# Up projection of an MLP: three of four hidden groups as seven quarter products instead of eight, input normalised first, residual parked in memory

## The chip, the cores and the metric

One core of a Trainium2 chip runs the whole program. The metric is the device time of one execution in microseconds (us). Three runs of the kernel before gave 1219.78, 1217.89 and 1219.12 us; their median is 1219.12 us.

## The reference

One decoder layer is computed in float32 for 512 prompt tokens and 8 samples of 8 tokens: a token mixer, a cross attention into 256 memory tokens, and a squared-ReLU MLP with 4096 hidden columns. The change is in the MLP and in what leads into it:

```python
x = x + rmsnorm(cross_attn(rmsnorm(x, g_pre_xa), mem_k, mem_v, w_xq, w_xo), g_post_xa)
hf = rmsnorm(x, g_pre_ffn)
x = x + rmsnorm(jnp.square(jax.nn.relu(hf @ w_up)) @ w_down, g_post_ffn)
```

`w_up` is 1024 x 4096 and `w_down` is 4096 x 1024; there are 576 tokens in all.

## The kernel before, in words

Activations lie transposed, features on the 128 partitions, as tiles `[128, 8, 576]`: 8 slices of 128 features, the 576 tokens in two halves of 288. Every float32 operand is split into a high part (a cast, `split` L92 on ACT) and a low part (the rest, L93 on DVE), and every product of a weight tile and an activation slice is three matmuls of 128 x 128 by 288 columns: high by high, low by high, high by low (`mm3`, L197 to L200). One weight tile `[128, 1024]` holds 8 such blocks, the whole depth of 1024 for 128 output columns, so it is worth 24 matmuls for one half of the tokens.

Weights come by a plan that is fixed when the program is built (L132 to L163). `wfetch` (L166) loads the next 512 KB tile into one of four `wraw` buffers through SP's queue; `wsplit` (L175) makes `wh` and `wl` in a ring of three buffers; `wnext` (L187) keeps two split tiles ready. Side work is written as generators that `tick` (L117) advances by a step after each stretch of matmuls. `project` (L375) computes one half of the tokens at a time, and keeps a few split tiles of the first half for the second (`keep`; `KEEP_FFN` is 4), so the others are loaded and split again. `gemm_m` (L208) computes both halves with each tile.

The cross attention's output projection (`w_xo`) runs by halves (L506 to L524). While its second half runs, `chain_xa(0)` (L511) turns the first half into the MLP's input: `residual` (L420) computes the post norm's factor (`rstd` L228: sums of squares by three small matmuls L223, a power on POOL L236, a diagonal L240, a broadcast matmul L247), scales (L429), adds the residual (L431), and writes `fh` and `fl`, the input times its gain but **not** divided by its own root mean square (L438, L439). Squared ReLU is homogeneous, so that division is made at the end: `vff` keeps what the last norm needs for it (L518, L519, used at L234 to L238). `chain_xa(1)` does the same for the second half while the MLP has begun on the first.

The MLP (L531 to L557) takes the 4096 hidden columns in four groups of 1024. Each group is an up projection (group 0 by halves through `project`, groups 1 to 3 through `gemm_m`) whose eviction `to_h` (L535) applies ReLU on ACT, the square on DVE (L538) and the split, then a down projection that is summed over the groups in `y3` (L555, L557). The last group's down projection runs by halves in `last` (L559), each followed by the post norm, the residual and the store. The tiles `fh`, `fl` carry the program's names `bh`, `bl` in the profile, and the hidden tiles `xh`, `xl`.

The order in which each engine's instructions stand is fixed at build time by a scheduler that works from this code; each engine then runs its own row in order and waits on semaphores.

Of the kernel before, what the change touches and what calls it, by code (L numbers as in the profile page):

```python
# [6 lines left out]
F32 = mybir.dt.float32  # L7
# [49 lines left out]
def decoder_step(ctx, tc, xT, memT, ktc, vc, s_gla, s_ret, w_in, w_ga, w_a2, w_mix, w_xq, w_xk, w_xv, w_xo,  # L57
                 w_up, w_down, vecs, cst, gam, y_out, mk_out, mv_out, sg_p, sr_p, sg_s, sr_s):
# [20 lines left out]
    vff = [[perm.tile([96, 3], F32, name=f"vff{i}{j}") for j in range(2)] for i in range(2)]  # L79
# [5 lines left out]
    wz = acta.tile([P, 256], F32R, name="wz")  # L85
# [78 lines left out]
    raws, ready, staying = [], [], []  # L164

    def wfetch():  # L166
        if plan:
            src, mode = plan.pop(0), RING
            if isinstance(src, tuple):
                src, mode = src  # L170
            raw = wp.tile([P, 1024], F32, name="wraw", bufs=N_RAW)
            nc.sync.dma_start(out=raw if len(src.shape) == 2 else raw.rearrange("p (k n) -> p k n", n=src.shape[2]), in_=src)
            raws.append((raw, mode))

    def wsplit():  # L175
        if raws:
# [25 lines left out]
    def gemm(ps, w, xh, xl, c, k0=0, k1=KT):  # L202

        wh, wl = w
        for k in range(k0, k1):
            mm3(ps, wh[:, k, :], wl[:, k, :], xh[:, k, c], xl[:, k, c], k == 0, k == KT - 1)

    def gemm_m(xh, xl):  # L208
        w = wnext()
        ps = gtile()  # L210
        gemm(ps[:, 0, :NH], w, xh, xl, hc(0))
        tick()
        gemm(ps[:, 1, :NH], w, xh, xl, hc(1))
        return ps[:, :, :NH]

# [12 lines left out]
    def rstd(ss, n, t, v=None):  # L228


        ms = meansq(ss, n, t, EPS if v is None else 0.0)
        rs = npool.tile([P, 4], F32, name="rs")
        if v is not None:
            nc.vector.tensor_tensor(out=ms, in0=ms, in1=v[1], op=ALU.mult)  # L234
            nc.vector.tensor_scalar(out=ms, in0=ms, scalar1=EPS, scalar2=None, op0=ALU.add)  # L235
        nc.gpsimd.tensor_tensor(out=rs[:t, :n], in0=ms, in1=mhalf[:t, :n], op=ALU.pow)  # L236
        if v is not None:
            nc.vector.tensor_tensor(out=rs[:t, :n], in0=rs[:t, :n], in1=v[0], op=ALU.mult)  # L238
# [129 lines left out]
    y2p = ctx.enter_context(tc.tile_pool(name="y2p", bufs=1))  # L368
# [51 lines left out]
    def residual(y, r, half, ss, ss2=None, g2=None, oh=None, ol=None, scale=None, done=None):  # L420

        c = hc(half)
        rs, dg = rstd(ss, 3, 96, scale)
# [84 lines left out]
    fh = actb.tile([P, KT, NT], F32R, name="bh")  # L508
    fl = actb.tile([P, KT, NT], F32R, name="bl")

    def chain_xa(half):  # L511

        ss2 = y2p.tile([P, 2, 384], F32, name="ss2")
        yield from residual((y2a, y2b)[half], rr, half, ss[half], ss2[:, :, :NH], V_PRE_FFN, fh, fl)

        def stats():
# [3 lines left out]
        yield from stats()  # L520

    side.append(chain_xa(0))
    project(ah, al, 1, to(y2b, V_POST_XA, ss[1]))
    drain()  # L524
    side.append(chain_xa(1))


    hp = ctx.enter_context(tc.tile_pool(name="hp", bufs=2))
    staying.append(ctx.enter_context(tc.tile_pool(name="keepf", bufs=KEEP_FFN)))
    y3 = None  # L530
    for g in range(4):  # L531
        hh = acta.tile([P, KT, NT], F32R, name="xh")
        hl = acta.tile([P, KT, NT], F32R, name="xl")

        def to_h(hv, lv, ps):  # L535
            r = hp.tile([P, 2, NH], F32, name="hr")
            nc.scalar.activation(r, ps, AF.Relu)  # L537
            nc.vector.tensor_tensor(out=r, in0=r, in1=r, op=ALU.mult)  # L538
            split(hv, lv, r)

        if g == 0:
            for half in range(2):
                c = hc(half)
                project(fh, fl, half, lambda b, ps, first: to_h(hh[:, 2 * b:2 * b + 2, c], hl[:, 2 * b:2 * b + 2, c], ps), keep=KEEP_FFN)
                drain()
        else:
            for k in range(KT):
                to_h(h2(hh[:, k, :]), h2(hl[:, k, :]), gemm_m(fh, fl))
        if g == 0:
            y3 = biga.tile([P, KT, NT], F32, name="y3", tag="biga")  # L550
        if g < 3:
            for k in range(KT):
                ps = gemm_m(hh, hl)
                if g == 0:
                    nc.scalar.copy(h2(y3[:, k, :]), ps)  # L555
                else:
                    nc.vector.tensor_tensor(out=h2(y3[:, k, :]), in0=ps, in1=h2(y3[:, k, :]), op=ALU.add)  # L557

    def last(half):  # L559
# [20 lines left out]
        project(hh, hl, half, evict, keep=KEEP_FFN, end=end)  # L580

        def done(kk, c):
            nc.sync.dma_start(out=y_out[:, kk, c], in_=res[:, kk, c])
        side.append(residual(yv, rr, half, s1, scale=vff[half], done=done))
# [647 lines left out]
```

## Time and profile before

| | |
|---|---|
| median of three runs | 1219.12 us (1217.89 to 1219.78) |
| profiled execution, its own time | 1221.61 us |
| its span, first to last instruction | 1219.9 us |
| mean granted TensorE clock | 0.989 |
| PE busy | 1190.6 us, 98% of the span, 9130 matmuls |
| DVE, ACT, POOL busy | 696.9, 527.7, 154.5 us (57%, 43%, 13%) |
| chain of work that ended last | PE 90%, DMA 4%, DVE 2%, ACT 2% |

The span is the profiled execution from its first to its last instruction; 1.7 us of its time lie around it. A matmul's busy time is its way through the array, so busy times of matmuls overlap, and PE's pace is read from the starts of neighbouring matmuls. Shares of busy time are means over stages, and the stages differ; the windows of single stages tell more.

### The profile page before, as it was taken

How to read it: one execution, taken by the hardware profiler on the slowest of the kernel's cores; microseconds unless marked ns; L12 is line 12 of the kernel's file. 1: busy time of each engine (PE TensorE's matmuls, PEld its weight loads, DVE VectorE, ACT ScalarE, POOL GpSimd, SP SyncE). 2: the span in 40 equal slices, each digit the busy share in tenths (PEclk: the TensorE clock that was granted, in tenths of full speed). 3: DMA queues.
4: the chain of work that ended last, by engine and by line, in shares of the span. 5: the costliest groups of instructions: out<-in, count | busy, mean ns of one | idle time of the engine just before them, and what ended most of it. 6: DMA issues, size and time to landing. Idle time of an engine off the chain costs nothing.

```text
span 1219.9 us, 22015 instructions
## 1 busy us (share of the span) xinstructions
PE 1190.6 (98%) x9130; PEld 1167.2 (96%) x9130; DVE 696.9 (57%) x1228; ACT 527.7 (43%) x944; POOL 154.5 (13%) x156
## 2 busy tenths in 40 slices
PE   8999999999999999999999998999999999999995
PEld 8999999999999999999999787999999999999995
DVE  6756667566757675768686443783224324333544
ACT  6624556534544364535564344653223213213431
POOL 0621213121312231221001000000000000000000
PEclk8999999999999999999999999999999999999998
DMA  8852323232324242423654766442222222222401
GB/s 265 262 187 89 125 87 117 82 123 87 126 79 128 77 126 75 138 87 112 207 161 148 246 197 231 163 139 70 87 78 79 87 87 87 76 80 87 139 12 67
DMA packets 60372, 149.45 MB, mean 123 GB/s; under 512 B 5520, under 2 KB 30224, under 8 KB 60144
## 3 DMA queue, kind: packets, MB, share of 16 engines
q1 hardware_dynamic: 60272, 148.04, 37.8%
q8 instruction: 72, 1.18, 0.4%
q14 instruction: 28, 0.23, 0.1%
HBM read 134.12 MB, written 13.89 MB: 121 GB/s over the span
## 4 chain that ended last, share of the span: by engine, by line
PE 90%; DMA 4%; DVE 2%; ACT 2%; issue 0%; POOL 0%; SPq 0%; POOLq 0%; DVEq 0%; ACTq 0%
PE psg L200 27%; PE psg L199 27%; PE psg L198 27%; DMA wraw<-in_w_xo 2%; PE psa L198 1%; PE psa L199 1%; PE psa L200 1%; DVE wl L93 1%; ACT wh L92 1%; PE pso L1056 1%; PE psa L773 1%; PE pso L899 1%; PE pso L900 1%; PE psa L901 1%; DMA wraw<-in_vc 1%; DMA wraw<-in_w_xq 1%
## 5 line engine op out<-in xcount | busy, mean ns | idle before, releaser
L198 PE MATMUL psg<-xh,wh 128*128 128x288 f32 x1808 | 538.1, 298 | 4.5 <-ACT wh L92 3.8
L199 PE MATMUL psg<-xh,wl 128*128 128x288 f32 x1808 | 534.6, 296 | 2.1 <-DVE wl L93 2.1
L200 PE MATMUL psg<-xl,wh 128*128 128x288 f32 x1808 | 534.1, 296 | 0.0
L198 PEld LDWEIGHTS psg<-xh,wh 128*128 128x128 f32 x1808 | 340.8, 189 | 7.2 <-ACT wh L92 5.3
L199 PEld LDWEIGHTS psg<-xh,wl 128*128 128x128 f32 x1808 | 341.1, 189 | 2.9 <-DVE wl L93 2.7
L200 PEld LDWEIGHTS psg<-xl,wh 128*128 128x128 f32 x1808 | 340.7, 189 | 0.9 <-DVE xl L93 0.9
L93 DVE TENSOR_TENSOR wl<-wraw,wh 128x1024 fp32r<-128x1024 f32 x189 | 233.5, 1237 | 110.7 <-ACT wh L92 109.9
L92 ACT CAST wh<-wraw 128x1024 fp32r<-128x1024 f32 x189 | 198.0, 1049 | 175.8 <-PE psg L200 126.2
L198 PE MATMUL psg<-bh,wh 128*128 128x288 f32 x640 | 189.3, 296 | 1.1 <-ACT wh L92 1.1
L199 PE MATMUL psg<-bh,wl 128*128 128x288 f32 x640 | 188.7, 295 | 0.0
L200 PE MATMUL psg<-bl,wh 128*128 128x288 f32 x640 | 188.7, 295 | 0.0
L198 PEld LDWEIGHTS psg<-bh,wh 128*128 128x128 f32 x640 | 120.0, 188 | 1.8 <-ACT wh L92 1.3
L199 PEld LDWEIGHTS psg<-bh,wl 128*128 128x128 f32 x640 | 120.0, 188 | 0.3 <-DVE wl L93 0.2
L200 PEld LDWEIGHTS psg<-bl,wh 128*128 128x128 f32 x640 | 120.0, 188 | 0.2 <-DVE bl L93 0.2
L236 POOL TENSOR_TENSOR rs<-ms,mhalf 96x3 f32<-96x3 f32 (+1 forms) x9 | 8.4, 936 | 538.9 <-DVE ms L235 408.9
L538 DVE TENSOR_TENSOR hr<-hr 128x576 f32<-128x576 f32 x32 | 24.2, 757 | 89.6 <-ACT hr L537 89.6
L537 ACT ACTIVATE hr<-psg 128x576 f32<-128x576 f32 x32 | 20.9, 652 | 108.2 <-PE psg L200 108.2
L557 DVE TENSOR_TENSOR y<-psg,y 128x576 f32<-128x576 f32 x16 | 12.1, 758 | 62.7 <-PE psg L200 62.7
L759 ACT COPY vt<-psg 128x512 f32<-128x512 f32 x16 | 9.4, 588 | 79.2 <-PE psg L200 79.2
L688 POOL TENSOR_TENSOR rs<-mv,mhalf 128x1 f32<-128x1 f32 (+1 forms) x40 | 26.8, 670 | 108.6 <-DVE mv L683 60.9
L761 DVE COPY vd<-psg 128x96 f32<-128x96 f32 x32 | 6.7, 252 | 52.1 <-ACT vt L759 52.1
L258 DVE TENSOR_TENSOR ss<-ss,sq 128x576 f32<-128x576 f32 x34 | 25.7, 755 | 16.7 <-ACT sq L257 16.3
(276 smaller groups left out, 1597.1 us busy)
## 6 DMA issues: line engine op xcount, KB each, us to landing
wraw<-in_w_in SPq DMA_DIRECT2D x64, 512.0 KB, 3.6
wraw<-in_w_up SPq DMA_DIRECT2D x34, 512.0 KB, 3.6
wraw<-in_w_down SPq DMA_DIRECT2D x34, 512.0 KB, 3.6
wraw<-in_ktc SPq DMA_DIRECT2D x16, 512.0 KB, 4.2
wraw<-in_vc SPq DMA_DIRECT2D x16, 512.0 KB, 5.7
wraw<-in_w_xq SPq DMA_DIRECT2D x14, 512.0 KB, 4.0
wraw<-in_w_xo SPq DMA_DIRECT2D x14, 512.0 KB, 5.6
wraw<-in_w_mix SPq DMA_DIRECT2D x12, 512.0 KB, 4.5
```

The costliest lines, as they stand in the source:

```text
L92: nc.scalar.copy(hi, src)
L93: nc.vector.tensor_tensor(out=lo, in0=src, in1=f32(hi), op=ALU.subtract)
L198: nc.tensor.matmul(out, ah, bh, start=first, stop=False)
L199: nc.tensor.matmul(out, al, bh, start=False, stop=False)
L200: nc.tensor.matmul(out, ah, bl, start=False, stop=last)
L258: eng.tensor_tensor(out=ss, in0=ss, in1=sq[:, :, :n], op=ALU.add)
L537: nc.scalar.activation(r, ps, AF.Relu)
L538: nc.vector.tensor_tensor(out=r, in0=r, in1=r, op=ALU.mult)
L688: nc.gpsimd.tensor_tensor(out=rs[:t], in0=mv[:t], in1=mhalf[:t, 0:1], op=ALU.pow)
L773: nc.tensor.matmul(sc[:, :P], kf[:, ci], qf[:, ci], start=True, stop=True)
L899: nc.tensor.matmul(so[:, :256], lq, s0h[:, j], start=False, stop=False)
L900: nc.tensor.matmul(so[:, :256], lq, s0l[:, j], start=False, stop=b == 7)
```

## The change

Groups 1 to 3 of the up projection no longer run as plain products. The tokens are cut into two halves and the depth of 1024 into two halves (even and odd slices), which gives the input quarters A11, A12, A21, A22; a pair of output tiles is cut likewise. A block of `sevenfold` computes one pair of output tiles (256 hidden columns) for all tokens from seven products of quarters, 12 matmuls each, where plain products take eight, and there are four blocks in each group. The products, in order, are A11, S1, S2, A12, S3, S4, A22, where S1 to S4 are sums of input quarters, made once by `sums_f` during group 0's down projection. The weights' sums are made for each block by `begin` and its units: four subtractions of 512 columns on DVE (L212) and three and a half splits (`p0`, `t`, `p1`, half of `p1`) in place of two. The output's sums are made partly by adding further products onto the same PSUM tile after ACT has copied what stands there (`p1`, `u2`, and `p5` for a tile that is used again), partly on DVE (`c11`, `c22`, `c12`).

The sums need input that is on one scale, so `chain_xa` now applies the whole pre-MLP norm before the MLP, and `vff` is gone. `fsh` and `fsl` (the split sums) take room, so the residual `res` is stored to `y_out` by `spill`, and loaded again as `res2` before the last down projection. `KEEP_FFN` is gone too: six tiles instead of two are loaded and split again in the second halves of group 0's up and of group 3's down projection. In group 0 the square moves to ACT and, for the first half, the low part of the hidden tile is made later (`lows`).

```diff
-    for g in range(4):
-        plan += keep(whole(w_up), KEEP_FFN) + rest(whole(w_up), KEEP_FFN) if g == 0 else whole(w_up, 4 * g)
-        plan += keep(whole(w_down, 12), KEEP_FFN) + rest(whole(w_down, 12), KEEP_FFN) if g == 3 else whole(w_down, 4 * g)
+    plan += whole(w_up) + rest(whole(w_up), 0) + whole(w_down)
+    for g in range(1, 4):
+        plan += seven(w_ups, 4 * (g - 1))
+        plan += whole(w_down, 4 * g) + (rest(whole(w_down, 12), 0) if g == 3 else [])
...
+    def begin():
+        while len(raws) < 2:
+            wfetch()
+        p0, p1 = (raws.pop(0)[0] for _ in range(2))
+        t = wp.tile([P, 1024], F32, name="wraw", bufs=N_RAW)
+        q0, q1, qt = halves(p0), halves(p1), halves(t)
...
+        units.extend([unit_a, lambda: ring(t), lambda: own(p1, 0, 1024),
+                      lambda: minus(q1[:, 0], q1[:, 0], qt[:, 0]), lambda: own(q1[:, 0], 2048, 512)])
+        minus(qt[:, 1], q1[:, 1], q0[:, 1])
+        minus(q0[:, 1], q0[:, 1], q0[:, 0])
+        minus(qt[:, 0], q1[:, 1], q0[:, 1])
+        wfetch()
...
+    def sevenfold(x, p1, p5, u2, c11, c22, c12, c21):
...
+        acc, b, c = atile()[:, :NH], otile()[:, :NH], gtile()[:, 0, :NH]
+        wa, wc, wb = (ready.pop(0) for _ in range(3))
+        prod(acc, wa, 0, "A11", True)
+        p1(acc)
+        while units:
+            wsplit()
+        wd = ready.pop(0)
+        prod(c, wa, 1, "S1", True)
+        p5(c)
+        if raws and raws[0][1] == SEVEN:
+            begin()
+        prod(acc, wc, 0, "S2", False)
+        wsplit()
+        u2(acc)
+        prod(b, wb, 0, "A12", True)
+        more()
+        c11(b)
+        prod(acc, wc, 1, "S3", False)
+        c22(acc)
+        prod(c, wb, 1, "S4", False)
+        c12(c)
+        more()
+        prod(acc, wd, 0, "A22", False)
+        more()
+        c21(acc)
...
-            nc.vector.reciprocal(vff[half][0], meansq(ss2[:, :, :NH], 3, 96))
-            nc.vector.tensor_tensor(out=vff[half][1], in0=vff[half][0], in1=vff[half][0], op=ALU.mult)
...
+    def chain_xa(half, tmp, tag):
+        q = slice(2 * half, 2 * half + 2)
+        ss2 = tmp.tile([P, 2, NH], F32, name="ss2", tag=tag)
+        yield from residual((y2a, y2b)[half], rr, half, ss[half], ss2, done=spill)
+        yield
+        rs, dg = rstd(ss2, 3, 96)
+        yield
+        bc = bcast(dg, 3, 96)
+        for j in range(4):
+            xn = tmp.tile([P, 2, NH], F32, name="xn", tag=tag)
+            for k in range(2):
+                g = V_PRE_FFN + 2 * j + k
+                nc.vector.scalar_tensor_tensor(out=xn[:, k], in0=res[:, 2 * j + k, hc(half)], scalar=vec[:, g:g + 1], in1=bc,
+                                               op0=ALU.mult, op1=ALU.mult)
+            split(fh[:, q, j], fl[:, q, j], xn)
+            yield
...
+            for b in range(4):
+                c1, c2 = (hp.tile([P, 2, NH], F32, name="hr") for _ in range(2))
+                def c22(ps):
+                    add(c2[:, 1], ps, c2[:, 1])
+                    nc.scalar.activation(c2[:, 1], c2[:, 1], AF.Relu)
+                def c12(ps):
+                    add(c1[:, 1], ps, c1[:, 1])
+                    nc.scalar.activation(c1, c1, AF.Relu)
+                    nc.scalar.activation(c1, c1, AF.Square)
+                    split(hh[:, 0:2, b], hl[:, 0:2, b], c1)
+                def c21(ps):
+                    nc.scalar.activation(c2[:, 0], ps, AF.Relu)
+                    nc.scalar.activation(c2, c2, AF.Square)
+                    split(hh[:, 2:4, b], hl[:, 2:4, b], c2)
...
+    res2 = fsp.tile([P, KT, NT], F32, name="res2", tag="fsh")
+    for half in range(2):
+        for k in range(0, KT, 2):
+            nc.sync.dma_start(out=res2[:, k:k + 2, hc(half)], in_=y_out[:, k:k + 2, hc(half)])
```

The instructions' new order is read at three places.

**ACT in the up projection of group 2.** Before, a tile of output asks for a ReLU out of PSUM (L537), a cast of a weight tile (`wh`), and a cast of the hidden tile (`xh`), and so on:

```order
L537 ACTIVATE hr_12777<-psg_12728 128x576
L92 CAST wh_12844<-wraw_12722 128x1024
L92 CAST xh_12720<-hr_12777 128x576
L537 ACTIVATE hr_12837<-psg_12788 128x576
L92 CAST wh_12904<-wraw_12782 128x1024
```

With the change, this is the stretch across the end of a block, from `c22`'s ReLU to the first weight cast of the block after (L712 is `c22`'s ReLU, L716 and L717 are `c12`'s, L721 and L722 `c21`'s, L725 the copies `p1` and `p5`, L726 the copy `u2`; `wq` is the buffer for `p1` and its half):

```order
L712 ACTIVATE hr_11922<-hr_11922 128x288
L92 CAST wq_10466<-wraw_11867 128x1024
L716 ACTIVATE hr_11921<-hr_11921 128x576
L721 ACTIVATE hr_11922<-psa_11929 128x288
L717 ACTIVATE hr_11921<-hr_11921 128x576
L722 ACTIVATE hr_11922<-hr_11922 128x576
L92 CAST hh_11919<-hr_11921 128x2x288
L92 CAST hh_11919<-hr_11922 128x2x288
L725 COPY hr_12053<-psa_12055 128x288
L92 CAST wq_10466<-wraw_11867 128x512
L725 COPY hr_12054<-psg_12057 128x288
L92 CAST wh_12104<-wraw_11965 128x1024
```

The first copy L725 is `p1` of the next block. It stands behind seven instructions of the block before, all of which wait, directly or through one another, for that block's last two products.

**DVE in the same block.** Before, a tile of output asked DVE for one low part of a weight tile, one square and one low part of the hidden tile. With the change one block (two tiles) asks for:

```order
L653 TENSOR_TENSOR hr_12054<-psa_12055,hr_12054 128x288
L653 TENSOR_TENSOR hr_12053<-psg_12057,hr_12053 128x288
L93 TENSOR_TENSOR wq_10466<-wraw_11983,wq_10466 128x1024
L212 TENSOR_TENSOR wraw_11983<-wraw_11983,wraw_12086 128x512
L212 TENSOR_TENSOR wraw_12211<-wraw_12108,wraw_12090 128x512
L212 TENSOR_TENSOR wraw_12090<-wraw_12090 128x512
L93 TENSOR_TENSOR hl_11920<-hr_12053,hh_11919 128x2x288
L93 TENSOR_TENSOR hl_11920<-hr_12054,hh_11919 128x2x288
L93 TENSOR_TENSOR wq_10466<-wraw_11983,wq_10466 128x512
L212 TENSOR_TENSOR wraw_12211<-wraw_12108,wraw_12090 128x512
L93 TENSOR_TENSOR wl_12230<-wraw_12090,wh_12229 128x1024
L93 TENSOR_TENSOR wl_12249<-wraw_12211,wh_12248 128x1024
```

The first two rows are `c22` and `c12`; the next block's `c11` and `c22` come right behind the last row, so they stand behind the low parts of two weight tiles (`wl`) that only the blocks after need.

**DVE ahead of the MLP, in the second half of `w_xo`.** Before, the low parts `bl` of the MLP's input follow each part of the residual at once:

```order
L431 TENSOR_TENSOR res_7479<-y2a_7483,res_7479 128x2x288 x2
L93 TENSOR_TENSOR wl_9663<-wraw_9619,wh_9662 128x1024
L439 SCALAR_TENSOR_TENSOR bl_9542<-res_7479,vec_79,bh_9541 128x288 x2
L258 TENSOR_TENSOR ss2_9568<-ss2_9568,sq_9653 128x2x288
L439 SCALAR_TENSOR_TENSOR bl_9542<-res_7479,vec_79,bh_9541 128x288 x2
```

With the change they stand behind a second set of statistics (L321, L325, L334, and a broadcast on PE):

```order
L321 TENSOR_TENSOR ss2_9567<-ss2_9567 128x288
L93 TENSOR_TENSOR wl_9793<-wraw_9712,wh_9792 128x1024
L325 TENSOR_SCALAR ms_9705<-psa_9700 96x3
L334 TENSOR_TENSOR dg_9709<-idn_81,rs_9707 96x288
L633 SCALAR_TENSOR_TENSOR xn_9744<-res_7475,vec_79,psa_9742 128x288 x2
L352 TENSOR_TENSOR ss_8956<-ss_8956,sq_9781 128x576
L633 SCALAR_TENSOR_TENSOR xn_9784<-res_7475,vec_79,psa_9742 128x288 x2
L93 TENSOR_TENSOR fl_9538<-xn_9744,fh_9537 128x2x288
```

Before, the first low part of the input stood two rows behind the first parts of the residual; now it stands behind all parts of the residual, all their sums of squares and the second statistics.

## Rows read from the trace of the kernel before

**Rows 1.** The page: busy time by engine, and the clock over 40 slices.

```profile
PE 1190.6 (98%) x9130; PEld 1167.2 (96%) x9130; DVE 696.9 (57%) x1228; ACT 527.7 (43%) x944; POOL 154.5 (13%) x156
...
PEclk8999999999999999999999999999999999999998
```

**Rows 2.** Windows: span, busy PE, PEld, DVE, ACT, POOL (instructions), PEclk, DMA share, GB/s.

```profile
769.00:794.00 25.00, 25.00 (x189) 24.72 (x188) 22.57 (x35) 19.74 (x34) 0.85 (x1) 1.00 0.42 129
820.00:845.80 25.80, 25.80 (x196) 25.80 (x195) 9.65 (x11) 8.24 (x11) 0.00 (x0) 1.00 0.18 59
896.70:947.70 51.00, 51.00 (x387) 51.00 (x386) 19.80 (x22) 16.71 (x23) 0.00 (x0) 1.00 0.27 83
947.70:998.70 51.00, 51.00 (x385) 50.79 (x385) 16.54 (x17) 9.51 (x10) 0.00 (x0) 1.00 0.27 84
```

**Rows 3.** Timeline of PE in group 1's up projection: first and last of 57 rows.

```profile
899.53 0.29 PE L200 MATMUL psg<-bl,wh 128*128 128x288 f32 x1
...
906.95 0.30 PE L199 MATMUL psg<-bh,wl 128*128 128x288 f32 x1
```

**Rows 4.** Groups by line and shape: busy, mean ns, then idle time before.

```profile
L93 DVE TENSOR_TENSOR wl<-wraw,wh 128x1024 fp32r<-128x1024 f32 x189 | 233.5, 1237 | 110.7 <-ACT wh L92 109.9
L92 ACT CAST wh<-wraw 128x1024 fp32r<-128x1024 f32 x189 | 198.0, 1049 | 175.8 <-PE psg L200 126.2 <-DMA wraw<-in_w_xo 13.5 <-DMA wraw<-in_w_xq 9.3
L258 DVE TENSOR_TENSOR ss<-ss,sq 128x576 f32<-128x576 f32 x34 | 25.7, 755 | 16.7 <-ACT sq L257 16.3
L93 DVE TENSOR_TENSOR s0l<-s,s0h 128x512 fp32r<-128x512 f32 x32 | 22.2, 694 | 0.0
L92 ACT CAST xh<-hr 128x576 fp32r<-128x576 f32 x32 | 21.6, 674 | 6.5 <-DVE hr L538 6.5
L92 ACT CAST s0h<-s 128x512 fp32r<-128x512 f32 x32 | 19.8, 619 | 13.8 <-PE pso L899 8.4 <-DMA s<-in_s_ret 3.3 <-DVE wl L93 1.2
L92 ACT CAST vh<-psa 128x256 fp32r<-128x256 f32 x32 | 11.9, 371 | 14.4 <-DVE kl L791 13.6 <-DVE kl L93 0.7
L257 ACT ACTIVATE sq<-res 128x576 f32<-128x576 f32 x12 | 8.2, 681 | 2.7 <-DVE res L431 2.3 <-DVE ss L258 0.4
L575 DVE TENSOR_TENSOR y<-psg,y 128x288 f32<-128x288 f32 x4 | 1.8, 458 | 6.1 <-PE psg L200 6.1
```

**Rows 5.** Timeline: two casts in a row on ACT; PE's last matmul and its reader.

```profile
790.03 2.00 ACT L92 CAST wh<-wraw 128x1024 fp32r<-128x1024 f32 x2
...
1204.91 0.29 PE L200 MATMUL psg<-xl,wh 128*128 128x288 f32 x1
1205.24 0.46 DVE L575 TENSOR_TENSOR y<-psg,y 128x288 f32<-128x288 f32 x1 [2.65 <-PE psg L200]
```

**Rows 6.** Timeline of `chain_xa(0)`: sums done, POOL's power, first scaled part.

```profile
767.44 0.46 DVE L221 TENSOR_TENSOR ss<-ss 128x288 f32<-128x288 f32 x1
769.04 0.85 POOL L236 TENSOR_TENSOR rs<-ms,mhalf 96x3 f32<-96x3 f32 x1 [35.02 <-DVE ms L225]
772.60 1.42 DVE L429 TENSOR_TENSOR y2a<-y2a,psa 128x576 f32<-128x576 f32 x2 [1.08 <-PE psa L247]
```

**Rows 7.** Chain of waits: a broadcast of the statistics on PE (start, us).

```profile
772.08 0.49 PE psa L247 x2
```

**Rows 8.** Timeline of the tail: the three small operations that use `vff`.

```profile
1207.62 0.16 DVE L234 TENSOR_TENSOR ms<-ms,vff 96x3 f32<-96x3 f32 x1
1207.81 0.17 DVE L235 TENSOR_SCALAR ms<-ms 96x3 f32<-96x3 f32 x1
...
1208.99 0.16 DVE L238 TENSOR_TENSOR rs<-rs,vff 96x3 f32<-96x3 f32 x1 [1.02 <-POOL rs L236]
```

**Rows 9.** Timeline and windows (columns as in rows 2) where PE waited for a weight tile.

```profile
697.16 0.40 PE L198 MATMUL psg<-xh,wh 128*128 128x288 f32 x1 [2.13 <-ACT wh L92]
...
700.00:704.00 4.00, 4.00 (x18) 3.95 (x17) 1.23 (x1) 1.05 (x1) 0.00 (x0) 0.50 0.34 117
744.00:752.00 8.00, 7.57 (x73) 5.73 (x72) 1.95 (x3) 2.61 (x5) 0.00 (x0) 1.00 0.79 258
```

More of the change, by code (lines that the diff above doesn't have):

```diff
@@ L418, in rr, with residual @@
         return res[:, kk, c]
[L420 removed]
+    def residual(y, r, half, ss, ss2=None, g2=None, oh=None, ol=None, done=None, res=res):
         c = hc(half)
[L423 removed]
+        rs, dg = rstd(ss, 3, 96)
         yield
@@ L522, in decoder_step, with quarters, x @@
[L522 to L529, printed above, removed]
+    fh = actb.tile([P, 4, 4, NH], F32R, name="fh", tag="bh")
+    fl = actb.tile([P, 4, 4, NH], F32R, name="fl", tag="bl")
+    def quarters(h, l):
+        def x(k, c):
+            q = (2 if c.start else 0) + k % 2
+            return h[:, q, k // 2], l[:, q, k // 2]
+        return x
@@ L530, in decoder_step, with xf7 @@
+    FQ = {"A11": (fh, fl, 0), "A12": (fh, fl, 1), "A22": (fh, fl, 3),
+          "S2": (fsh, fsl, 0), "S4": (fsh, fsl, 1), "S3": (fsh, fsl, 2), "S1": (fsh, fsl, 3)}
+    def xf7(n):
+        h, l, q = FQ[n]
+        return h[:, q], l[:, q]
     y3 = None
     for g in range(4):
[L532 to L539, printed above, removed]
+        hh = acta.tile([P, 4, 4, NH], F32R, name="hh", tag="xh")
+        hl = acta.tile([P, 4, 4, NH], F32R, name="hl", tag="xl")
@@ L541, in decoder_step, with to_h @@
         if g == 0:
+            lows = []
             for half in range(2):
-                c = hc(half)
-                project(fh, fl, half, lambda b, ps, first: to_h(hh[:, 2 * b:2 * b + 2, c], hl[:, 2 * b:2 * b + 2, c], ps), keep=KEEP_FFN)
-                drain()
-        else:
[L547 to L550, printed above, removed]
+                def to_h(b, ps, first):
+                    q = slice(2 * half, 2 * half + 2)
+                    r = hp.tile([P, 2, NH], F32, name="hr")
+                    nc.scalar.activation(r, ps, AF.Relu)
+                    nc.scalar.activation(r, r, AF.Square)
+                    nc.scalar.copy(hh[:, q, b], r)
+                    low = lambda: add(hl[:, q, b], r, f32(hh[:, q, b]), ALU.subtract)
+                    if half == 0:
+                        lows.append(low)
+                    else:
+                        low()
+                project(quarters(fh, fl), None, half, to_h)
+                drain()
+                while lows:
+                    lows.pop(0)()
@@ new lines, in decoder_step @@
+            y3 = bigb.tile([P, KT, NT], F32, name="y3", tag="res")
+            side.append(sums_f())
+            wq.append(biga.tile([P, 4608], F32R, name="wq", tag="biga"))
+        else:
+            for b in range(4):
+                c1, c2 = (hp.tile([P, 2, NH], F32, name="hr") for _ in range(2))
+                def c22(ps):
[10 more added lines that the diff above has]
+                    split(hh[:, 2:4, b], hl[:, 2:4, b], c2)
+                sevenfold(xf7, lambda ps: nc.scalar.copy(c1[:, 0], ps), lambda ps: nc.scalar.copy(c2[:, 1], ps),
+                          lambda ps: nc.scalar.copy(c1[:, 1], ps), lambda ps: add(c1[:, 0], ps, c1[:, 0]), c22, c12, c21)
@@ L578, in end @@
             nc.scalar.activation(y, y, AF.Copy, scale=vec[:, V_POST_FFN + k:V_POST_FFN + k + 1])
-        project(hh, hl, half, evict, keep=KEEP_FFN, end=end)
+        project(quarters(hh, hl), None, half, evict, end=end)
         def done(kk, c):
-            nc.sync.dma_start(out=y_out[:, kk, c], in_=res[:, kk, c])
-        side.append(residual(yv, rr, half, s1, scale=vff[half], done=done))
+            nc.sync.dma_start(out=y_out[:, kk, c], in_=res2[:, kk, c])
+        side.append(residual(yv, lambda kk, c: res2[:, kk, c], half, s1, done=done, res=res2))
     last(0)
```

132 lines of the change are left out of this document (100 added, 32 removed).

## The prediction

> **What bounds the kernel now.** I read the page's busy times first, then the windows of single stages, then the timeline of PE inside one stage. PE is busy for 98% of the span and its granted clock stays at the upper of its two levels, 2.4 GHz, in nearly every slice [rows 1]; DVE stands at 57% and ACT at 43%. In the windows of the MLP [rows 2] PE is never idle, while DVE works 19.80 us and ACT 16.71 us of the 51.00 us of an up projection, and 16.54 and 9.51 us of a down projection. So the MLP is worth its number of matmuls times their pace. The pace is in the starts of 57 neighbouring matmuls [rows 3]: 7.42 us over 56 steps, 0.1325 us each. A product of 12 matmuls takes 1.59 us, a block of seven 11.13 us, and the eight that it replaces 12.72 us.
>
> **The sum, part by part.**
>
> *Fewer matmuls.* Each of 12 blocks (three groups of four) drops one product: 144 matmuls less, 144 x 0.1325 = **-19.1 us**, if PE never waits for what the blocks add elsewhere. The rest of the working is about that "if".
>
> *What a block adds.* DVE: three low parts of 1024 columns (1.237 each), one of 512 (0.694), four subtractions of 512 (0.694, taken from the only subtraction of that size shown), three additions of 288 out of PSUM (0.458), two low parts of 576 (0.755, the nearest row of that size) [rows 4]: 10.1 us of 11.13. ACT: three casts of 1.049, one of 0.619, three copies of 288 out of PSUM and one ReLU of 288 (0.40 each, from 256 columns in 0.371), one ReLU of 288 out of PSUM (0.40), one ReLU and two squares of 576 (0.681), two casts of 576 (0.674) [rows 4]: about 9.2 us. Both fit, with a tenth and a sixth to spare, so order decides, and I follow it through one block. Time 0 is the end of a block's last product, A22.
>
> *ACT's wait, in every block but a group's first.* A reader of PSUM starts 0.33 us after the start of the last matmul [rows 5], 0.20 after its slot. The product ahead, S4, ended at -1.59, so the cast of `p1` starts at -1.39 and ends at -0.34; `c12`'s ReLU ends at 0.34, `c21`'s at 0.74, two squares at 2.10, two casts at 3.44, and the copy of the next block's A11 at 3.84. PE has done A11 and S1 by 3.18, and S2 adds onto the tile being copied: a wait of 0.66 us. But neighbouring instructions on ACT overlap, two casts of 1.05 in 2.00 us [rows 5]; with 0.10 off at each handover after `c21`'s ReLU, which can't start before A22 is visible at 0.20, the copy ends at 3.20 and the wait is about zero. Dependent ones (ReLU, square, cast) may not overlap; I take the middle, 0.3 us. Nine blocks: **+2.7 us**, bounds 0 and 5.9. A group's first block has DVE and ACT at leisure, its weights being made during the down projection ahead: nothing.
>
> *DVE's place in the same loop.* Behind that copy ACT casts half of `p1` (4.46), DVE takes its low part and the third subtraction (5.9), ACT casts `t` (7.0), DVE takes its low part (8.2), and only then `c11` and `c22` (9.2). A22 adds onto the tile that `c22` reads and is due at 9.54 plus the wait: met, with some 0.5 us in hand. Everything else (S3 behind `u2`, S4 behind `p5`, A12 behind `p1`'s low part at 0.9) has over a microsecond. The loads have cover too: a block asks for two tiles, the second issued when `p0`'s low part ends at about 7, and wanted 5.6 us later.
>
> *A group's end.* The down projection's first tile wants the last block's hidden tile after 18 matmuls, 2.4 us; `c21`'s ReLU, two squares and two casts end between 2.4 and 3.2: 0.3 us each, three times, **+0.9** (0 to 2.4).
>
> *The norm ahead of the MLP.* Two broadcasts more on PE, 0.49 each [rows 7]; the sums of squares that `vff` needed become those of the new norm, so their number stays. **+1.0.** The scaling `xn` takes the place of the old low part, and a true low part of 576 comes on top, eight times 0.755 on a DVE that is busy for 22.57 of 25.00 us here [rows 2]. Now the waits. DVE's sums are ready at 767.44 and the first scaled part starts at 772.60 [rows 6]: one set of statistics, with POOL's power of 0.85 in it, costs 5.2 us, of which DVE idles some 2.9. From 772.60 to the new sums there stand four scalings and four additions of 576, three sums, one of the other half's, a sum of halves and four weight low parts (0.755, 0.46, 1.237; some 0.07 overlap each): ready at 784.5, where PE arrives at 783.7: 0.8. The factor comes 0.3 late. The first half's last low part ends near 798.2, PE wants it at 796.6: 1.6. The second half's chain of eight holds one weight tile back by 1.0. That is 3.7, and the old code's own statistics there cost PE about 1.0 of waits and small matmuls that go: **+2.7** beside the broadcasts, bounds 0 and 6.5.
>
> *The tail.* Three operations between the last sums and the factor go, 0.19 from start to start [rows 8]: **-0.6**, all on the path.
>
> *At nothing.* Eight more tiles loaded and split: 1.24 us of DVE each in windows like 820 to 846, where DVE works 9.65 of 25.80 us and DMA stands at 0.18 [rows 2]; without that cover a tile costs PE up to 1 us. Storing `res` puts four DMAs ahead of the next weight tiles on SP, twice; they wait for DVE's residual, some 2 us later than the tiles were issued, and the first tile has over 10 us until it is wanted. Loading `res2` waits for the last reader of `fsh` and stands ahead of the seventh tile of the last down projection, 19 us before its use. The sums of the input: 16 additions of 288, 8 of 576 and 8 low parts, 19 us of DVE in group 0's down projection, where DVE has 34 free in a window of that kind [rows 2].
>
> Sum: -19.1 + 2.7 + 0.9 + 1.0 + 2.7 - 0.6 = **-12.4 us**. The profiled execution took 1221.6 us (span 1219.9 and 1.7 around it), 2.5 above the median of 1219.12; against the median the forecast is **1206.7 us**.
>
> **The rivals.**
>
> *All covered.* The waits in the blocks, at the groups' ends and ahead of the MLP vanish, because ACT overlaps everywhere and the scheduler placed the statistics early: -19.1 + 1.0 - 0.6 = -18.7, **1200.4 us**. For it speaks ACT's overlap [rows 5], against it the DVE window ahead of the MLP.
>
> *Upper bounds.* Full durations on ACT, 0.66 and some handovers on top, 0.8 x 9 = 7.2; 2.4 at the ends; 6.0 ahead of the MLP: -19.1 + 7.2 + 2.4 + 1.0 + 6.0 - 0.6 = -3.1, **1216.0 us**.
>
> *The loop through DVE decides (slower).* From A22 through ACT's seven instructions, two casts and five DVE instructions back to `c22`, a loop takes 9.2 us, plus A22's 1.6: 10.8, just under the 11.13 of PE. It crosses between the engines nine times, and a handover that costs 0.2 us more each time makes it 12.6. A block then lasts longer than the 12.72 us of before from 1.9 us extra on. At 13.0 us: 12 x (13.0 - 11.13) = 22.4 in place of the 2.7: -19.1 + 22.4 + 0.9 + 1.0 + 2.7 - 0.6 = +7.3, **1226.4 us**. For it: DVE has a tenth free, and `c22` stands behind two weight low parts. Against it: handovers in the rows read are under 0.1 us.
>
> *The clock.* Where PE stood idle for 2.13 us ahead of one matmul and waited again behind it, the granted clock fell to 0.50, the lower level of 1.2 GHz, and 18 matmuls took 4.00 us [rows 9], 0.22 each. Where PE was busy for 7.57 of 8 us it stayed at 1.00 [rows 9]. My waits of 0.3 us in 11 are of the second kind. If they were of the first, the 1008 matmuls of the blocks would cost 0.09 more each, **1297 us**. The Trainium skill, "TensorE: Matmul & The Clock Gate", section "A second HAM failure mode: psum-queue depth-cycling", speaks against this change: a kernel that goes through PSUM banks with short idle times between groups of matmuls had its clock going down and up, and lost throughput by it. By that rule the last figure would come true; the trace, with the clock at 1.00 through the window with short gaps, does not bear it out.
>
> **How the numbers follow.** My forecast 60%, all covered 15%, upper bounds 12%, the loop 10%, the clock 3%. The range leaves out the last two and a little of each end: from all covered to just above the upper bounds, 1200 to 1217 us. A measurement of this kernel tells some 0.2% (2.4 us) from no change. Faster: the first two and most of the third, 0.83. Slower: the last two, 0.13. Within 0.2%: 0.04.
>
> **What would show it.** In the changed profile: 7200 matmuls of 288 columns instead of 7344, PE's clock at 1.00 through the MLP, blocks 11.2 to 11.8 us apart; S2's first matmul waiting for ACT's L725 by 0 to 0.7 us in three blocks of four, and A22 for nothing. Ahead of the MLP, waits for the statistics and `fl` of some 3 us together. The forecast is wrong if A22 waits for DVE's L653 in most blocks, if blocks lie over 12 us apart, or if the DMA of `w_ups` shows among the waits.

## The result: 1209.2 us, and the profile after

The changed kernel took 1209.22 us (median of 4 runs, 1208.38 to 1209.86), the kernel before, beside it, 1219.45 us (4 runs): a ratio of 0.9919, 95% interval 0.9907 to 0.993. It is faster by 10.2 us; the forecast was 1206.7 us. The profiled execution took 1208.38 us, its span is 1206.7 us.

The page, busy times and clock [rows 1]:

```profile
PE 1176.0 (97%) x8990; PEld 1150.4 (95%) x8990; DVE 773.9 (64%) x1344; ACT 590.9 (49%) x1056; POOL 157.3 (13%) x158
...
PEclk9999999999999999999999989999999999999998
```

PE is still the engine that is never done, with fewer matmuls; DVE and ACT have more to do. Windows from stage to stage (columns as in [rows 2]): w_xo's second half from the first half's statistics on, up projection 0, up 1, down 1, the last down up to its last sums, the tail.

```profile
766.21:791.97 25.76, 24.95 (x186) 24.29 (x185) 21.20 (x33) 15.79 (x23) 1.71 (x2) 1.00 0.46 152
791.97:848.36 56.39, 54.41 (x403) 53.01 (x401) 41.82 (x58) 33.73 (x47) 2.56 (x2) 1.00 0.53 162
899.39:945.07 45.68, 45.33 (x338) 44.85 (x337) 31.54 (x42) 30.00 (x51) 0.00 (x0) 1.00 0.35 105
945.07:996.23 51.16, 51.16 (x386) 51.02 (x385) 21.77 (x25) 11.80 (x15) 0.00 (x0) 1.00 0.23 73
1138.86:1194.45 55.59, 53.06 (x395) 51.93 (x393) 32.19 (x43) 27.91 (x43) 0.85 (x1) 1.00 0.42 139
1194.45:1206.70 12.25, 1.42 (x8) 0.88 (x8) 6.03 (x10) 0.02 (x1) 0.85 (x1) 0.64 0.29 96
```

Set out by stage, from the starts of PE's rows in the four traces that matter (us; "scaled input" and "both edits" are the experiments e4_unnorm and e9_unnorm_copy below):

| stage | before | changed | scaled input | both edits |
|---|---|---|---|---|
| start to w_xo's first statistics | 768.18 | 766.21 | 766.79 | 766.11 |
| w_xo, second half | 24.13 | 25.76 | 24.13 | 24.15 |
| up 0 | 53.47 | 56.39 | 52.79 | 52.81 |
| up 1 to 3 | 152.64 | 137.15 | 136.93 | 134.81 |
| down 0 to 2 | 153.39 | 153.35 | 153.34 | 153.31 |
| down 3 to the last sums | 54.91 | 55.59 | 55.60 | 55.60 |
| tail | 13.2 | 12.2 | 13.2 | 13.3 |
| span | 1219.9 | 1206.7 | 1202.8 | 1200.1 |

The three up projections give 15.5 us. The stretch ahead of the MLP and up 0 take 4.55 back, the last down 0.7; the tail gives 1.0. The first line, 2 us of the difference between these two traces, is the same code, whose time varies from run to run: the changed trace is 1.1 us ahead after the first 30 us (granted clock 0.89 in the one and 1.00 in the other), and gains the other 0.9 between 690 and 768 us, where PE waits for weight tiles in both. This is 2 of the 3 us by which the distance of the traces (13.2 us) exceeds that of the medians (10.2); the third is taken up in the section on the prediction.

What PE waited for from the end of the attention on (the waits of 764 to 1210 us: total, times, longest; the view lists waits of more than 0.15 us):

```profile
PE psg L251 <- DVE wl L93: 2.1, 3, 0.9
PE psa L341 <- DVE dg L334: 2.0, 2, 1.7
PE psa L323 <- DVE ss L761: 1.5, 1, 1.5
PE psa L280 <- ACT hr L725: 1.2, 3, 0.4
PE psg L250 <- DVE y L759: 0.6, 1, 0.6
PE psg L252 <- DVE fl L93: 0.6, 1, 0.6
PE psg L250 <- ACT fh L92: 0.2, 1, 0.2
```

In the seven-product blocks one kind of wait is listed, S2 for L725 (ACT's copy of `p1`), three times; A22 is not in the list. The other waits belong to the norm ahead of the MLP (`fl`, `fh`, one `dg`, two of the `wl`) and to the last down projection and its tail (the third `wl` among them). Blocks of group 1 start at 899.39, 910.58, 921.92 and 933.26 us and the group ends at 945.07: 11.19, 11.34, 11.34, 11.81 us, with 11.20 for seven products of 1.60. The last is the longest. PE's timeline there:

```profile
936.46 0.29 PE L280 MATMUL pso<-fh,wq 128*128 128x288 f32 x1
937.11 0.40 PE L280 MATMUL psa<-fsh,wh 128*128 128x288 f32 x1 [0.35 <-ACT hr L725]
```

In the second block the same wait is too short for the list, but S2 starts 0.05 us after the end of the copy:

```profile
913.38 0.40 ACT L725 COPY hr<-psa 128x288 f32<-128x288 f32 x1
...
913.83 0.40 PE L280 MATMUL psa<-fsh,wh 128*128 128x288 f32 x1
```

The chain of work that ended last, around the start of the last block of group 2 (start, us, piece):

```profile
1023.19 0.62 DVE wq L93
1023.82 3.82 DMA wraw<-in_w_down
1027.68 0.04 issue
1027.72 1.06 ACT wh L92
...
1030.03 0.38 DVE hr L653
1030.41 0.02 issue
1030.43 0.69 ACT hr L716
...
1033.69 0.31 ACT hr L725
1034.00 0.04 issue
1034.04 1.87 PE psa L280 x12
```

The prediction had not seen this. The first tile of the coming down projection is loaded into a buffer of the ring that comes free only when DVE has made the last low part of the third block's weights (1023.19, done by 1023.82). ACT's cast of that tile stands in ACT's row ahead of `c22`'s and `c12`'s ReLUs. It waits for the load until 1027.72, everything behind it in ACT's row is late, and `p1`'s copy, last in the row, holds S2.

### The profile page after: what moved, and what is told of

Read it like the earlier page. It is cut to its first block, busy times and chain, and to the rows that moved or that the text cites. A ratio compares the mean times of both kernels' runs of the same rounds, so it can differ in the third digit from the quotient of the medians.

```text
span 1206.7 us, 22033 instructions
## 1 busy us (share of the span) xinstructions
PE 1176.0 (97%) x8990; PEld 1150.4 (95%) x8990; DVE 773.9 (64%) x1344; ACT 590.9 (49%) x1056; POOL 157.3 (13%) x158
## 4 chain that ended last, share of the span: by engine, by line
PE 87%; DVE 6%; DMA 3%; ACT 3%; issue 1%; POOL 0%; POOLq 0%; DVEq 0%; SPq 0%; ACTq 0%
PE psg L251 23%; PE psg L250 23%; PE psg L252 23%; PE psa L280 4%; PE psg L280 2%; PE psa L250 1%; PE psa L251 1%; PE psa L252 1%; DVE wl L93 1%; PE pso L280 1%; DMA wraw<-in_w_xo 1%; PE pso L1240 1%; ACT wh L92 1%; DMA wraw<-in_w_down 1%; DVE res L525 1%; PE psa L957 1%
## 5 line engine op out<-in xcount | busy, mean ns | idle before, releaser
L250 PE MATMUL psg<-xh,wh 128*128 128x288 f32 x1296 | 387.2, 299 | 3.2 <-ACT wh L92 3.2
L251 PE MATMUL psg<-xh,wl 128*128 128x288 f32 x1296 | 383.9, 296 | 2.3 <-DVE wl L93 2.3
L252 PE MATMUL psg<-xl,wh 128*128 128x288 f32 x1296 | 383.5, 296 | 0.0
L251 PEld LDWEIGHTS psg<-xh,wl 128*128 128x128 f32 x1296 | 244.9, 189 | 3.2 <-DVE wl L93 3.1
L250 PE MATMUL psg<-hh,wh 128*128 128x288 f32 x512 | 151.8, 297 | 0.7 <-DVE y L759 0.6
L251 PE MATMUL psg<-hh,wl 128*128 128x288 f32 x512 | 150.8, 295 | 0.3 <-DVE wl L93 0.3
L252 PE MATMUL psg<-hl,wh 128*128 128x288 f32 x512 | 150.8, 295 | 0.0
L250 PEld LDWEIGHTS psg<-hh,wh 128*128 128x128 f32 x512 | 96.1, 188 | 1.6 <-issue 1.1
L251 PEld LDWEIGHTS psg<-hh,wl 128*128 128x128 f32 x512 | 96.1, 188 | 0.6 <-DVE wl L93 0.6
L250 PE MATMUL psg<-bh,wh 128*128 128x288 f32 x128 | 38.4, 300 | 1.1 <-ACT wh L92 1.1
L251 PE MATMUL psg<-fh,wl 128*128 128x288 f32 x128 | 38.1, 298 | 0.9 <-DVE wl L93 0.9
```

What stands on the lines that cost most here:

```text
L250: nc.tensor.matmul(out, ah, bh, start=first, stop=False)
L251: nc.tensor.matmul(out, al, bh, start=False, stop=False)
L252: nc.tensor.matmul(out, ah, bl, start=False, stop=last)
```

## The experiments

The kernel before ran beside each group of them: 1220.08 us (11 runs) for e1 to e4, 1219.39 (7) for e5 to e8, 1218.37 (7) for e9 and e10.

**e1_plain: the seven products undone.**

```diff
-        plan += seven(w_ups, 4 * (g - 1))
+        plan += whole(w_up, 4 * g)
...
-                sevenfold(xf7, ...)
+                ps = gemm_m(quarters(fh, fl), None)
```

> Groups 1 to 3 of the up projection as plain products again (eight products of quarters' worth, so 7344 matmuls of 288 columns), without the sums on VectorE; all else of the change stays (input normalised first, residual in memory, no kept weight tiles). My theory: the whole gain sits in these three projections. Each goes from 45.7 us back to 50.9, the stretch ahead of the MLP, the downs and the tail stay as in the changed kernel: 1209.2 + 15.5 = 1224.7 us, about 5 us slower than the kernel before. Rival (part of the gain came from elsewhere, such as the start of the program or the residual in memory): below 1219 us.

1225.33 us (4 runs), ratio 1.0044 (1.0029 to 1.0059). Up 1 is back to the DVE, ACT and PE time of [rows 2]:

```profile
901.77:952.76 50.99, 50.99 (x387) 50.99 (x385) 19.80 (x22) 16.73 (x23) 0.00 (x0) 1.00 0.28 84
```

w_xo and up 0 keep their new waits (56.38 us for up 0). So the gain sits in the three projections alone, and the rest of the change costs 5.3 us in the medians.

**e2_order: A12 ahead of S2.**

```diff
-        prod(acc, wc, 0, "S2", False)
-        wsplit()
-        u2(acc)
         prod(b, wb, 0, "A12", True)
-        more()
         c11(b)
+        prod(acc, wc, 0, "S2", False)
+        wsplit()
+        u2(acc)
+        more()
```

> Product A12 is made ahead of S2 in each block, so that ScalarE's copy of p1 has 1.6 us more before S2 adds onto its tile. My theory: what a block takes above its seven products (0.15 us in blocks 1 and 2, 0.6 in block 3 of a group) is only this copy; blocks go to 11.2 us, three projections save 2.7 us together: about 1206.5 us, and PE waits nowhere in them for L725. Rival (the loop through VectorE sets the block's length): the wait comes back at S3 or A22, blocks stay at 11.34 us and the time at 1209.

1208.29 us (4 runs), ratio 0.9905 (0.9892 to 0.9917): not to be told from the changed kernel, and the projections stayed at 45.68, 45.67 and 45.68 us. L725 is gone from the waits, as expected. But S3 now follows S2 on the same PSUM tile with nothing between, and `u2` has to copy that tile first. PE's and ACT's timelines at S3:

```profile
905.88 0.29 PE L280 MATMUL psg<-fsh,wq 128*128 128x288 f32 x1
906.13 0.40 PE L280 MATMUL psa<-fsh,wh 128*128 128x288 f32 x1
...
905.68 0.40 ACT L726 COPY hr<-psa 128x288 f32<-128x288 f32 x1 [1.86 <-PE psa L280]
```

The scheduler put four matmuls of S4 in the hole, and each block still pays 0.22 us. My edit was a bad one: the four products on one tile need the three others between them. As a test of the loop through VectorE it says nothing.

**e3_spare: a buffer of its own for the first down tile.**

```diff
-        plan += whole(w_down, 4 * g) + ...
+        plan += [(w_down[4 * g][:, 0], SPARE)] + whole(w_down, 4 * g)[1:] + ...
...
-            raw = wp.tile([P, 1024], F32, name="wraw", bufs=N_RAW)
+            raw = spare[0].tile([P, 1024], F32, name="wsp") if mode == SPARE else wp.tile(...)
```

> The first down weight tile of groups 1 to 3 is loaded into a buffer of its own, so its load need not wait until a buffer of the ring comes free, and ScalarE's cast of it in the middle of the last hidden block waits for no DMA. My theory: the last block of each group comes down from 11.81 to the 11.34 us of its neighbours, 0.47 x 3 = 1.4 us: about 1207.8 us; S2 of the last block waits 0.1 to 0.2 us for L725 as in the others. Rival (the last block is long because VectorE has one more weight tile there, not for the load): no change, block at 11.8 us, 1209.2.

1207.56 us (6 runs), ratio 0.9905 (0.989 to 0.9921). The time alone can't tell it from the changed kernel; the stages can: up 1 to 3 take 45.16 us each, 0.52 to 0.62 less, all of it in the last block (the others stay at 11.19, 11.34 and 11.34), and the waits list nothing between 903 and 1141 us. The cast now waits for PE, which still reads the older weight tile in its output buffer, and for no load:

```profile
1030.81 1.05 ACT L92 CAST wh<-wsp 128x1024 fp32r<-128x1024 f32 x1 [1.62 <-PE psa L280]
```

That confirms the chain read above. This profile lost 1.5 us in up 0, to the clock (last section).

**e4_unnorm: the input scaled by the gain only, its norm taken into the last one, as before the change.**

```diff
-        yield from residual(..., ss2, done=spill)
+        yield from residual(..., ss2, V_PRE_FFN, fh, fl, done=spill)
         yield
-        rs, dg = rstd(ss2, 3, 96)
...
+        nc.vector.reciprocal(vff[half][0], meansq(ss2, 3, 96))
+        nc.vector.tensor_tensor(out=vff[half][1], in0=vff[half][0], in1=vff[half][0], op=ALU.mult)
```

> The input of the MLP is no longer normalised first: as in the kernel before it is only scaled by the gain, and the row's factor comes in at the last norm; the seven products, the residual in memory and the reloaded weight tiles stay. My theory: the 4.55 us that the stretch from the statistics of the first half to the end of the first up projection grew by come from the norm (two broadcasts, its statistics and the longer chain on VectorE that also delays weight tiles); they go, and the tail gets 0.6 to 0.9 us back: about 1205.5 us, with w_xo's second half at 24.1 and the first up projection at 53.5 us. Rival (the two waits for weight low parts of 0.8 and 0.95 us come from the eight tiles that are now loaded and split twice): they stay, and only 2.9 less 0.7 us is won: about 1207 us.

1203.68 us (4 runs), ratio 0.9862 (0.9845 to 0.988). That is less than the 1205.5 expected, in part since up 0 took 0.7 us less than in the kernel before: 0.58 of it is a wait for a broadcast's diagonal (`dg`) that the trace of before has in up 0 and this one has not. w_xo's second half is at 24.13 us, up 0 at 52.79, the tail at 13.2. What PE waits for between 764 and 1210 us is now:

```profile
PE psa L347 <- DVE dg L340: 2.3, 1, 2.3
PE psa L324 <- DVE ss L758: 1.5, 1, 1.5
PE psa L281 <- ACT hr L722: 0.9, 3, 0.4
PE psg L251 <- DVE y L756: 0.6, 1, 0.6
PE psg L252 <- DVE wl L94: 0.3, 1, 0.3
```

The two waits of 0.79 and 0.95 us for weight low parts are gone although all eight tiles are still loaded and split twice: the rival falls, the norm's longer work on DVE had delayed those tiles. The residual kept in memory stays in this kernel, and no stage shows a cost of it. The last down (55.60 us, 0.7 over before) has the reloaded tiles and the residual's load both new, and the trace points at the tiles: 0.3 us is a wait for `wl`, the low part of a tile that the kernel before had kept, which DVE made behind the eight rows that scale and add the first half's residual. With the two slow matmuls around it this is 0.6 us. The same wait in the changed kernel:

```profile
1179.18 0.40 PE L251 MATMUL psg<-hh,wl 128*128 128x288 f32 x1 [0.32 <-DVE wl L93]
```

**e5_sub1, e6_sub3, e10_sub6: more work for VectorE in the blocks.** N is 2, 4 and 7: the subtraction is made again with the same numbers.

```diff
-        minus(qt[:, 0], q1[:, 1], q0[:, 1])
+        for _ in range(N):
+            minus(qt[:, 0], q1[:, 1], q0[:, 1])
```

> Each block makes one of VectorE's four subtractions of 512 columns twice (the same numbers again, 0.62 to 0.69 us more for VectorE in a block). My theory: VectorE has room, since its last sum ahead of A22 ends 0.95 us before A22 starts in the changed kernel's trace; blocks stay at 11.34 us, time 1209 to 1210. Rival (the loop from A22 through ScalarE and VectorE back to A22 sets the block): every block grows by the 0.6 us, 9 to 12 times: 1214.5 to 1216.5 us, and A22 waits for L653.

> The same subtraction four times instead of once: three more, 1.9 to 2.1 us of VectorE in each block. My theory: VectorE's work of a block goes from 10.1 to about 12.2 us and passes the 11.2 us of the seven products, so now VectorE does set the block: 12.0 to 12.4 us each in all but a group's last, 0.7 to 1.1 us x 9: 1215.5 to 1219 us, with A22 (or the product after it) waiting for L653. Were VectorE far from setting anything, it would stay at 1209 to 1211.

> The subtraction of the experiments with one and three extra ones is made six times more in each block, 3.7 us of VectorE. Three more cost nothing, so I now hold that VectorE has 1.9 us to spare in a block (9.5 of 11.34 us busy in the changed kernel) and that the loop decides from there on: the two blocks of a group whose weights are made under other blocks grow by some 1.8 us each, 3 x 2 x 1.8 = 11 us, 1217 to 1221 us, with A22 or S3 waiting for L653 or a low part. Rival (VectorE isn't in the loop at all, the scheduler puts the extra work where it has time): 1207 to 1210.

One extra: 1208.97 us (0.9915, 0.99 to 0.993), up 1 to 3 at 45.27 us. Three: 1207.47 us (0.9902, 0.9888 to 0.9917), 45.1 to 45.3 us. Six: 1209.3 us (0.9914, 0.9892 to 0.9936). The first was as expected; my theory missed the other two. For three the time lies below what I had put for a VectorE that sets nothing (1209 to 1211), for six the rival held. A window of up 2 with three extra, against 32.30 us of DVE in the changed kernel there:

```profile
994.34:1039.43 45.09, 45.09 (x339) 44.87 (x338) 35.62 (x49) 28.96 (x50) 0.00 (x0) 1.00 0.31 98
```

DVE has 9.5 us left in 45. And the scheduler does not keep the order when VectorE's work grows: with three extra, the cast of the down tile no longer stands ahead of `c22`, and ACT copies `p1` (L726 here) between the two casts of the hidden tile instead of behind them. The last blocks came out shorter, 11.2 us in groups 1 and 2 instead of 11.8 and 11.9:

```profile
1030.29 0.66 ACT L92 CAST hh<-hr 128x576 fp32r<-128x576 f32 x1
...
1031.44 0.39 ACT L726 COPY hr<-psa 128x288 f32<-128x288 f32 x1
1031.71 0.68 ACT L92 CAST hh<-hr 128x576 fp32r<-128x576 f32 x1
```

With six extra, the last block's products wait, but the scheduler puts matmuls of the down projection (L251 to L253) between them. Group 1's up and down together, in e10_sub6 and in the changed kernel:

```profile
898.96:996.25 97.29, 97.18 (x722) 96.03 (x721) 67.66 (x91) 42.35 (x65) 0.00 (x0) 1.00 0.28 91
```

```profile
899.39:996.23 96.84, 96.49 (x722) 95.88 (x721) 53.32 (x67) 41.80 (x65) 0.00 (x0) 1.00 0.28 88
```

14.3 us more of DVE cost 0.45 us. So these runs changed the order of the rows along with the load, and measure both together: in none of the orders that ran does a loop through VectorE set the block, and a fixed order with more load was not tried.

**e7_copy_dve: VectorE copies `p1`.**

```diff
-  lambda ps: nc.scalar.copy(c1[:, 0], ps)
+  lambda ps: nc.vector.tensor_copy(c1[:, 0], ps)
```

> The copy of p1 out of PSUM is made by VectorE instead of ScalarE, whose row of ReLUs, squares and casts stands ahead of it. My theory: S2's waits (0.05 to 0.1 us in blocks 1 and 2, 0.5 in block 3 of each group) go, VectorE has the 0.4 us to spare: blocks at 11.2 to 11.25 us, 45.0 us for a projection, 2 us saved: about 1207.2 us. Rival (the loop through VectorE is as tight as ScalarE's row): the copy on VectorE delays c22 and A22 by as much as it saves, 1209 to 1211.

1206.47 us (4 runs), ratio 0.9899 (0.9884 to 0.9913). By the stages it is as expected: 45.04, 44.88 and 44.88 us, 2.35 us less in the three, no wait listed in them, and the load that comes late costs nothing any more, since `p1` no longer stands behind it. Up 1, and VectorE's copy:

```profile
899.28:944.32 45.04, 45.04 (x339) 44.86 (x338) 32.90 (x46) 28.69 (x47) 0.00 (x0) 1.00 0.34 106
```

```profile
1020.19 0.45 DVE L725 COPY hr<-psa 128x288 f32<-128x288 f32 x1
```

**e8_unnorm_spare: e4 and e3 together.** The edits are those shown above.

> Two edits together: the MLP's input only scaled, its norm taken into the last one, and the buffer of its own for the first down tile of groups 1 to 3. If the two gains are independent, as I hold: 1203.7 less 1.4 to 1.6 us, about 1202.2 us, with up projections 1 to 3 at 45.1 to 45.2 us and the first at 52.8. Rival (with VectorE freed ahead of the MLP the load no longer comes late in any case): 1203.7.

1202.02 us (4 runs), ratio 0.9861 (0.9845 to 0.9878). Up 0 took 52.79 us, up 1 to 3 45.16, 45.17 and 45.16 (45.61, 45.61 and 45.71 in e4): the gains add, in the stages; the ratios of e4 and e8 can't be told apart.

**e9_unnorm_copy: e4 and e7 together.** The edits are those shown above.

> The two edits that gained most, together: the MLP's input only scaled (its norm taken into the last one) and the copy of p1 made by VectorE. They touch different stretches, so I expect the gains to add: 1203.7 - 0.8 x 3 = about 1201.3 us, with PE waiting for nothing in the three projections (44.9 us each) and its clock at 1.00 through the first up projection. Rival (with the row on ScalarE shorter, the waits come back elsewhere): 1203.7.

1201.04 us (4 runs), ratio 0.9851 (0.9825 to 0.9877): 1.5% below the kernel before and the lowest median that ran, though its interval overlaps those of e4 and e8. No wait of PE is listed between 764 and 1131 us. w_xo's second half, up 0 and up 2:

```profile
766.11:790.26 24.15, 24.15 (x184) 23.86 (x183) 21.25 (x32) 16.99 (x28) 0.85 (x1) 1.00 0.58 185
790.26:843.07 52.81, 52.79 (x401) 52.45 (x400) 36.04 (x53) 34.21 (x50) 0.85 (x1) 1.00 0.51 163
990.27:1035.14 44.87, 44.87 (x338) 44.85 (x337) 33.63 (x47) 28.14 (x46) 0.00 (x0) 1.00 0.36 106
```

## Why the prediction was right, and where its terms were off

The mechanism held: PE's number of matmuls decides, the blocks are a little longer than their products because S2 waits for ACT's copy of `p1`, and the norm ahead of the MLP costs what is left. Term by term:

- *Fewer matmuls, -19.1.* It came to -18.2: three projections without a wait take 44.8 us (28 products of 1.60; e7 and e9 show 44.87 to 45.04) in place of 50.88. A product took 1.60 us in the blocks and not the 1.59 of [rows 3].
- *S2's wait, +2.7.* Right in sum, by luck, since 0.3 was the middle between 0 and 0.66; wrong in shape. 11.19, 11.34, 11.34 and 11.81 us are 0.9 above the products, 2.7 for three groups; but the second and third block (1 and 2 in the expectations, which count from 0) lose 0.14 each and the last 0.61. I had made all three alike, since I counted ACT's instructions and not what they wait for: the load behind the cast (e3).
- *The groups' ends, +0.9.* Nothing: downs 1 and 2 take 51.16 us, and those of before 51.13. Together with the first term, two errors of 0.9 cancel; that is why, by luck, the projections came out at -15.5, the sum of the three terms to a tenth.
- *Ahead of the MLP, +3.7.* 4.55, a miss of 0.9. PE's idle time there grew from 0.58 to 2.79 us, where the sum had +2.7 of waits, and its busy time by 2.3, where it had +1.0. The sets of small sums stay four, where I let the old ones' go, and two broadcasts come on top, 0.72 and 0.75 us each where I had taken 0.49 from [rows 7]; a matmul behind a wait takes 0.40 instead of 0.29. The waits came elsewhere than forecast: none is listed for the new sums (0.8 in the sum), 0.79 and 0.95 us are for weight low parts. The working of those sums has a slip: the rows it lists add up to 13.3 us behind 772.60, not to the 11.9 that 784.5 means. The changed trace has three weight low parts there, not four, and takes 11.9 us (770.64 to 782.51). e4 shows that all of it is the norm's: without the norm ahead of the MLP the 4.55 are gone.
- *The tail, -0.6.* -1.0 in this pair of traces. The three operations are 0.58 of PE's wait, as forecast. The rest is the clock, and chance: in the trace of before the granted clock had fallen to 0.50 by the time PE made the last broadcast, and it took 1.33 us; in the changed kernel's trace it was still at 1.00 and the broadcast took 0.75. In the other seven profiles with the same code there it took 1.06 to 1.33, and the tail 12.5 to 12.8 us. Before, changed, and e2:

```profile
1209.69 1.33 PE L247 MATMUL psa<-dg,idn 96*128 96x288 f32 x2 [2.31 <-DVE dg L240]
```

```profile
1196.85 0.75 PE L341 MATMUL psa<-dg,idn 96*128 96x288 f32 x2 [1.73 <-DVE dg L334]
```

```profile
1196.71 1.33 PE L341 MATMUL psa<-dg,idn 96*128 96x288 f32 x2 [1.73 <-DVE dg L334]
```

- *At nothing.* Right for the store of the residual and the sums of the input (downs 0 to 2 unchanged). Not for the last down, +0.7, of which a reloaded tile's low part is 0.6 (e4).

Of the rivals, the loop through VectorE fell: three more subtractions in a block don't lengthen it, in the order that the scheduler then chose. Its working took every row at its full duration, in a fixed order; DVE's rows follow each other by 0.60 us where one takes 0.69, and the scheduler moves what would be late. The upper bounds were added up with 6.0 ahead of the MLP where the term's own bound was 6.5; that would have made them 1216.5. The clock rival did not come true in the blocks, and a small piece of it came where I had not put it (below).

The forecast was 2.5 us below the measured median. The terms above make up 1.1 of it: -11.3 us in the stages that changed, against -12.4. The kernel before was 0.3 us slower in this comparison than in the runs the sum was set against, and 1.1 us is left between the stages of one pair of traces and the medians. An estimate from the eight profiles that normalise first explains most of that: their tails are 0.4 us longer in the mean than in this trace, and three of them lose 1.5 us to the clock in up 0, which is 0.6 in the mean.

## What to carry to other kernels

When an instruction is last in an engine's row, ask of each one ahead of it what it waits for, not only how long it takes: here a prefetch's cast, waiting for its load, delayed the one copy on which the next product hung, and moving that copy to the engine with time to spare (e7) was worth 2.35 us, where the waits list only 1.2 for it. A change of several parts should be run with each part undone: the seven products were worth 15.5 us, and the norm that came along gave 4.5 of them back without need. The section on the change says that the sums need input on one scale, but in exact arithmetic the output's sums take the mixture of tokens out again whatever their scale: a factor per token passes through ReLU, square and both products and can come in at the last norm, as the kernel before and e4 have it. Where a scheduler orders the rows, an added load is not an experiment on a fixed order; read the new order before reading the time.

## What the hardware showed that was not expected

The granted clock fell at the start of up 0 in three of the eight profiles that normalise the input first (e3, e5, e6), for some 3 us each, and up 0 took 57.88 to 57.93 us instead of 56.38: 1.5 us. What PE did before it is the same in all eight, a wait of 0.17 and one of 0.56 us close together; why the clock fell in three of them and not in five stays open. e3's timeline and its windows of 1 us:

```profile
797.86 0.40 PE L250 MATMUL psg<-fh,wh 128*128 128x288 f32 x1 [0.17 <-ACT fh L92]
...
798.95 0.40 PE L252 MATMUL psg<-fl,wh 128*128 128x288 f32 x1 [0.56 <-DVE fl L93]
```

```profile
798.00:799.00 1.00, 0.44 (x3) 0.20 (x3) 1.00 (x3) 0.00 (x0) 0.00 (x0) 1.00 0.06 16
...
800.00:801.00 1.00, 1.00 (x8) 1.00 (x8) 0.56 (x3) 0.87 (x1) 0.39 (x1) 0.62 0.91 344
801.00:802.00 1.00, 1.00 (x6) 1.00 (x6) 1.00 (x1) 0.00 (x0) 0.46 (x1) 0.50 0.60 184
```

Six matmuls in a microsecond at 0.50, the lower level of 1.2 GHz, where PE was never idle. Single waits of 0.79 and 0.95 us elsewhere were followed by no fall, and neither were S2's 0.35 and 0.45 us; the kernels with the scaled input, which have no such pair of waits, show none here in three profiles. So the kernel that normalises first pays 1.5 us in some of its executions, which may be part of why e4 gained 5.5 us in the median and 3.9 between its profiled execution and that of the changed kernel. The Trainium skill, "TensorE: Matmul & The Clock Gate", section "A second HAM failure mode: psum-queue depth-cycling", warns of short idle times between groups of matmuls that take the clock down and up again. This pair of waits is of that kind in its shortness, at 1.5 us, though PE waited for the two parts of its input (`fh`, `fl`) and the cause of the fall is not shown. The waits in the blocks, one in 11 us, were not followed by any fall, and the rival's 1297 us, which keeps the clock at its lower level through all the blocks, was far off.
